# Stage ends of a one-core fp32 block: split weights a block ahead, last rows by halves of the tokens, 1/rms with priority, Sqrt's table loaded elsewhere

## The chip, the core and the metric

One NeuronCore of a Trainium2 chip runs the whole program. The time is device microseconds of one launch. The core's engines are PE (TensorE, matmuls; its weight loads are listed as PEld), DVE (VectorE), ACT (ScalarE), POOL (GpSimd) and SP (SyncE, which here issues DMAs). Each works through its own list of instructions in order, and waits where an operand of an instruction is not there yet.

## What is computed

Two layers on 256 latent tokens of width 2048. Layer 0 mixes tokens with a bidirectional RWKV-7 scan, which also reads 256 context tokens; layer 1 with a Hyena long convolution whose filters come from a small sine network. Behind each mixer and each MLP stands a root-mean-square norm, then the residual.

```python
def rms_norm(x, g):
    return x * lax.rsqrt(jnp.mean(x * x, axis=-1, keepdims=True) + NORM_EPS) * g

for i in range(2):
    h = modulate(rms_norm(x, norm_g[i, 0]), mod[:, 0], mod[:, 1])
    y = rwkv_mixer(h, hc, ...) if i == 0 else hyena_stream(h, ...)
    x = x + mod[:, 2] * rms_norm(y, norm_g[i, 1])
    h = modulate(rms_norm(x, norm_g[i, 2]), mod[:, 3], mod[:, 4])
    x = x + mod[:, 5] * rms_norm(squared_relu_mlp(h, mlp_up[i], mlp_down[i]), norm_g[i, 3])

# in hyena_filters, for L = 256 positions:
filt = (z @ f_w4).reshape(L, 2, HY_ORDER, D) * window
```

`rwkv_mixer` ends in a product with `w_o` (2048x2048), `hyena_stream` in one with `out_w`. `mod` is `silu(c) @ ada_w + ada_b`.

## The kernel before

All is fp32. Each operand of a product is split in two (ACT casts the high part, DVE subtracts for the low part; `split_into`), and each product is three matmuls (`mm3`: high·high, high·low, low·high). Names that end in h and l are these halves: `wh`, `wl` of a streamed weight, `w4h`, `w4l` of the filters' last weights, `hfh`, `hfl` of a filter block.

**Order of work.** The program is written as straight Python; every instruction is recorded (`call`, L53) and a scheduler then orders each engine's list from costs, dependencies and priorities. `tc.high_priority(n)` moves what stands in its block up by n. In the scan the order is pinned as written. Along time: projections (to about 600 us), the scan in eight groups (to 1421), `w_o` with its `resid` (to 1575), layer 0's MLP (to 2312) and `resid`, Hyena (to 2849) and `resid`, layer 1's MLP (to 3606) and `resid` to the output.

**Filters** (`filters`) fill PE's gaps in the scan's last group, 1290 to 1421. A unit is a column block dc (4 of 512) and an order o (2): eight units, 0 to 7. In a unit, for e = 0, 1 and token half tt = 0, 1: three matmuls of `zs`/`zd` with `w4` into an `sg` buffer; DVE multiplies by the window into `hf`; ACT casts `hfh`; DVE subtracts `hfl`; then `second` transforms them (matmuls with the DFT tables into `fl`), ACT copies `fl` to `ko`, SP stores `ko` to `spec`. The window of a column block (`win`, one buffer) is loaded for the next block when the last `hf` of a block is done. The weights of unit i are split when unit i begins.

**Streamed products.** `gemm_tok` computes 128 tokens by 512 columns per PSUM tile (column block n, token half tt), with K in blocks of four k; `w_o`, `mlp_down` and `out_w` use it. `evac` copies a tile to `o` (or adds to it; `y` in Hyena) on DVE, and `square_rows` sums its squares on ACT (`ysq`, into `ss`). `gemm_ws` has the weights' columns as output rows; in its lead mode four PSUM tiles share the K blocks, and `mlp_up` and Hyena's first product use it; there `evu` multiplies a tile by `rstd` into `nt`.

**resid** adds `ss` over n (DVE), takes Sqrt (ACT) and the reciprocal (DVE), and builds `dg`, a diagonal of 1/rms (DVE). PE multiplies `o` by `dg` (L450), which also transposes; `add` adds this to x and prepares the next stage's operands.

Beside all this `ada_run` computes `mod` from `ada_w` (`aw` tiles scaled on ACT, summed on POOL and DVE into `acc`), and `ada_scan` does some of it on PE in the scan, with the small tiles `wide` and `pick`.

Of the kernel before, what the change touches and what calls it, by code (L numbers as in the profile page):

```python
# [69 lines left out]
class Kern:  # L70
# [104 lines left out]
    def gemm_ws(self, W, K, ms, x, ntok, evac, lead=False):  # L175

        nk = K // P
        if lead:
            ps = [[self.mm.tile([P, 512], F32, name="mm") for _ in range(2)] for _ in range(2)]
            for k0 in range(0, nk, 4):  # L180
                w = [self.load_split(W[k0 * P : (k0 + 4) * P, m0 * P : (m0 + 2) * P].rearrange("(k p) n -> p k n", p=P), 4, 256)
                     for m0 in ms[:2]]
                for k in range(4):
                    for j in range(2):
                        for i in range(2):
                            self.mm3(ps[j][i][:, :ntok], self.cut(w[j][k], slice(i * P, (i + 1) * P)), x(k0 + k),
                                     k0 + k == 0, k0 + k == nk - 1)
                self.tick(self.rate)
            for j in range(2):
                for i in range(2):  # L190
                    evac(ms[j] + i, ps[j][i][:, :ntok])
            ms = ms[2:]
        for m0 in ms:
            ps = [self.mm.tile([P, 512], F32, name="mm") for _ in range(2)]
            for k0 in range(0, nk, 8):
                src = W[k0 * P : (k0 + 8) * P, m0 * P : (m0 + 2) * P].rearrange("(k p) n -> p k n", p=P)
                w = self.load_split(src, 8, 256)
                for k in range(8):
                    for i in range(2):
                        s = slice(i * P, (i + 1) * P)  # L200
                        self.mm3(ps[i][:, :ntok], self.cut(w[k], s), x(k0 + k),
                                 k0 + k == 0, k0 + k == nk - 1)
                self.tick(self.rate)
            for i in range(2):
                evac(m0 + i, ps[i][:, :ntok])

    def gemm_tok(self, W, x, evac, lead=False, stages=None):

        for ns in ((0, 1), (2,), (3,)) if lead else ((0,), (1,), (2,), (3,)):
            ps = {(n, tt): self.mm.tile([P, 512], F32, name="mm") for n in ns for tt in range(2)}  # L210
            for k0 in range(0, KT, 4):
                if stages and len(ns) > 1:
                    stages(k0)
                for n in ns:
                    w = self.load_split(W[k0 * P : (k0 + 4) * P, n * 512 : (n + 1) * 512].rearrange("(k p) n -> p k n", p=P), 4, 512)
                    for k in range(k0, k0 + 4):
                        for tt in range(2):
                            self.mm3(ps[n, tt], self.cut(x(k), slice(tt * P, (tt + 1) * P)), w[k - k0], k == 0, k == KT - 1)
                    self.tick(self.rate)
            for n in ns:  # L220
                for tt in range(2):
                    evac(n, tt, ps[n, tt])

    def square_rows(self, ss, y, n, tt, pool):

# [113 lines left out]
    def ada_scan(self, n, pool):  # L339


        nc = self.nc
        wide = pool.tile([P, KT, 32], F32, name="wide", bufs=1)
        nc.vector.memset(wide, 0.0)
        nc.vector.tensor_copy(wide[:, :, 0], self.sc2[:, 0, :])
        pick = pool.tile([P, 2], F32, name="pick", bufs=1)
        nc.vector.memset(pick, 0.0)
        for j in range(4):
            nc.vector.tensor_tensor(pick, pick, self.ident[:, 32 * j : 32 * j + 2], op=ALU.add)
        todo = [(layer, ch, i, half, k4) for layer, ch, i in itertools.islice(self.ada_todo, n) for half in range(2) for k4 in range(4)]  # L350

        def load(u):
            layer, ch, i, half, k4 = todo[u]
            w = pool.tile([P, 4, 256], F32, name="aw", bufs=2)
            c0 = ch * D + i * 512 + half * 256
            nc.sync.dma_start(w, self.I["ada_w"][layer, k4 * 512 : (k4 + 1) * 512, c0 : c0 + 256].rearrange("(a p) n -> p a n", p=P))
            return w

        def finish(layer, ch, i, half, ps):
            rows = pool.tile([P, 256], F32, name="rows", bufs=1)  # L360
            nc.scalar.copy(rows, ps)
            yield
            tp = self.sg.tile([P, 2, 2], F32, name="sg")
            for b in range(2):
                self.product(tp[:, b], rows[:, b * P : (b + 1) * P], pick, start=True, stop=True)
            c = 4 * i + 2 * half
            nc.vector.tensor_tensor(self.mod[:, layer, ch, c : c + 2], tp[:, :, 0], self.col("ada_b", layer * 96 + ch * 16 + c, 2), op=ALU.add)

        nxt = load(0)
        tail = iter(())  # L370
        for u, (layer, ch, i, half, k4) in enumerate(todo):
            w, nxt = nxt, load(u + 1) if u + 1 < len(todo) else None
            for _ in tail:
                pass
            if k4 == 0:
                ps = self.mm.tile([P, 256], F32, name="mm")
            for j in range(4):
                self.product(ps[32 * j : 32 * j + 32], wide[:, 4 * k4 + j, :], w[:, j], start=k4 == 0, stop=k4 == 3, tile_position=(0, 32 * j))
            if k4 == 3:
                tail = finish(layer, ch, i, half, ps)  # L380
                next(tail)
            yield
        for _ in tail:
            pass
# [40 lines left out]
    def resid(self, x, y, ss, layer, gi, ch, pool, nxt=None):  # L425
# [9 lines left out]
            for c in (L, L + 1):  # L435
                self.split_into(hi[:, :, c], self.mod[:, nxt[0], nxt[2], :], lo[:, :, c])

        for n in range(1, 4):
            nc.vector.tensor_tensor(ss[:, 0, :], ss[:, 0, :], ss[:, n, :], op=ALU.add)
        nc.scalar.activation(ss[:, 1, :], ss[:, 0, :], AF.Sqrt, bias=self.eps[:, 0:1], scale=1.0 / D)  # L440
        nc.vector.reciprocal(ss[:, 1, :], ss[:, 1, :])
        dg = pool.tile([P, 2, P], F32, name="dg", bufs=1)
        for tt in range(2):
            nc.vector.tensor_scalar(dg[:, tt], self.ident, ss[:, 1, tt : tt + 1], None, op0=ALU.mult)

        def add(k):
            pt = self.sg.tile([P, L], F32, name="sg")
# [30 lines left out]
    def filters(self, es):  # L478
# [46 lines left out]
        def load(i):  # L525
            dc, o = divmod(i, 2)
            if dc < 4:
                w4 = p2.tile([P, 512], F32, name="w4")
                for b in range(2):
                    c0 = (b * 2 + o) * D + dc * 512  # L530
                    nc.sync.dma_start(w4[64 * b : 64 * b + 64, :], I["f_w4"][0, :, c0 : c0 + 512])
                w4s.append(w4)
# [7 lines left out]
        def window(dc):  # L540
            if dc < 4:
                self.win = p2.tile([P, 2, 512], F32, name="win", bufs=1)
                nc.sync.dma_start(self.win, I["window"][:, dc * 512 : (dc + 1) * 512].rearrange("(a p) d -> p a d", p=P))

        window(0), load(0), skip(0)

        def first(dc, o, e, put):

            if not e:
                w4 = w4s.pop(0)  # L550
                self.w4 = split2(w4)
                load(2 * dc + o + 1)
            for tt in range(2):
                ps = self.sg.tile([P, 512], F32, name="sg")
                self.mm3(ps, self.cut(zz[e], slice(tt * P, (tt + 1) * P)), self.w4, True, True)
                hf = p2.tile([P, 512], F32, name="hf", bufs=3)
                nc.vector.tensor_tensor(hf, ps, self.win[:, tt, :], op=ALU.mult)
                if o and e and tt:
                    window(dc + 1)
                if e == 0 and tt == 0:  # L560
                    nc.vector.tensor_tensor(hf[0:1, :], hf[0:1, :], self.sk, op=ALU.add)
                    skip(2 * dc + o + 1)
                hh = p2.tile([P, 512], F32R, name="hfh", bufs=4)
                hfl = p2.tile([P, 512], F32R, name="hfl", bufs=4)
                put.append(self.split_into(hh[:], hf[:], hfl[:]))
                yield

        def split2(x):
            return self.split_into(p2.tile([P, 512], F32R, name="w4h")[:], x[:], p2.tile([P, 512], F32R, name="w4l")[:])

        def second(dc, o, e, hl):

# [851 lines left out]
    def rwkv_out(self, xp):  # L1424
        nc, tc = self.nc, self.tc
        with tc.tile_pool(reuse_waits="tile", name="oy", bufs=16) as oy, tc.tile_pool(reuse_waits="tile", name="op", bufs=1) as op:
# [7 lines left out]
            o = {(n, tt): op.tile([P, 512], F32, name=f"o{n}{tt}") for n in range(4) for tt in range(2)}  # L1434
            ss = op.tile([P, 4, 2], F32, name="ss")

            def ev(n, tt, ps):
                nc.vector.tensor_copy(o[n, tt], ps)
                self.square_rows(ss, o, n, tt, op)
# [43 lines left out]
            self.resid(x, o, ss, layer, 3, 5, mp, None if layer else (1, 0, 0))  # L1483

    AW = 6
    PRT = 1
    PRA, PRH = 100, 200
    MIXV = 3
    XB = 3
# [7 lines left out]
    PRI, PRJ = 200, 100  # L1497
    NEGV = 0
    SLACK = 0
    PRB = 200  # L1500
    LPOOL = 2
    FX = 3
# [332 lines left out]
```

## Time and profile before

| | |
|---|---|
| median of 3 runs | 3630.55 us (3610.51 to 3632.46) |
| profiled execution, its own time | 3626.62 us |
| its span, first to last instruction | 3623.9 us |
| mean granted TensorE clock | 0.965 |
| PE busy | 3349.5 us, 92% of the span |
| DVE, ACT, POOL busy | 2474.2 (68%), 1740.7 (48%), 551.9 us (15%) |
| DMA | 836.78 MB, mean 231 GB/s |

Shares are of the span. A time such as 1428.56 is counted from the span's start. A wait names the instruction that stood still and what released it; the engine behind a `<-` is that releaser.

### The profile page before, as it was taken

How to read it: one execution, taken by the hardware profiler on the slowest of the kernel's cores; microseconds unless marked ns; L12 is line 12 of the kernel's file. 1: busy time of each engine (PE TensorE's matmuls, PEld its weight loads, DVE VectorE, ACT ScalarE, POOL GpSimd, SP SyncE). 2: the span in 40 equal slices, each digit the busy share in tenths (PEclk: the TensorE clock that was granted, in tenths of full speed). 3: DMA queues.
4: the chain of work that ended last, by engine and by line, in shares of the span. 5: the costliest groups of instructions: out<-in, count | busy, mean ns of one | idle time of the engine just before them, and what ended most of it. 6: DMA issues, size and time to landing. Idle time of an engine off the chain costs nothing. (4 is left out here: it accounts for less than half of the span.)

```text
span 3623.9 us, 74582 instructions
## 1 busy us (share of the span) xinstructions
PE 3349.5 (92%) x30598; PEld 2912.4 (80%) x30598; DVE 2474.2 (68%) x3787; ACT 1740.7 (48%) x3069; POOL 551.9 (15%) x576
## 2 busy tenths in 40 slices
PE   7798877989999878999999999999999899999999
PEld 3376666878888756798988889899997798989897
DVE  5888675777777755587777776587787685555554
ACT  4444344444554544444434335576564664435343
POOL 2632221111111000000000002044441540000000
PEclk9989988999999989999999999999999999999999
DMA  9668798888899735688888887476665776555553
GB/s 328 203 211 268 238 293 253 272 267 272 272 281 276 224 126 168 202 257 288 255 271 277 283 264 240 158 238 214 213 211 176 241 251 197 178 189 182 192 181 126
DMA packets 587806, 836.78 MB, mean 231 GB/s; under 512 B 39551, under 2 KB 373280, under 8 KB 587464
## 3 DMA queue, kind: packets, MB, share of 16 engines
q1 hardware_dynamic: 556360, 718.76, 62.0%
q0 software_dynamic: 31104, 113.26, 9.9%
q8 instruction: 239, 3.92, 0.4%
q14 instruction: 103, 0.84, 0.1%
HBM read 777.31 MB, written 54.59 MB: 230 GB/s over the span
## 5 line engine op out<-in xcount | busy, mean ns | idle before, releaser
L53 DVE TENSOR_TENSOR wl<-w,wh 128x1024 fp32r<-128x1024 f32 (+1 forms) x716 | 919.6, 1290 | 541.1 <-ACT wh L53 537.8
L53 ACT CAST wh<-w 128x1024 fp32r<-128x1024 f32 (+1 forms) x716 | 737.7, 1043 | 728.8 <-PE mm L111 416.4
L111 PE MATMUL mm<-hxh,wh 128*128 128x258 f32 x2816 | 805.3, 287 | 13.2 <-DVE nt L53 11.4
L111 PE MATMUL mm<-hxh,wl 128*128 128x258 f32 x2816 | 803.9, 286 | 5.5 <-DVE wl L53 5.5
L111 PE MATMUL mm<-hxl,wh 128*128 128x258 f32 x2816 | 801.1, 285 | 0.0
L111 PEld LDWEIGHTS mm<-hxh,wh 128*128 128x128 f32 x2816 | 536.3, 191 | 17.4 <-DVE nt L53 13.5
L111 PEld LDWEIGHTS mm<-hxh,wl 128*128 128x128 f32 x2816 | 536.0, 190 | 8.5 <-DVE wl L53 7.2
L111 PEld LDWEIGHTS mm<-hxl,wh 128*128 128x128 f32 x2816 | 538.6, 191 | 1.8
L322 POOL TENSOR_TENSOR acc<-acc,aw 128x512 f32<-128x512 f32 x180 | 274.2, 1523 | 1360.7 <-ACT aw L53 1259.3
L111 PE MATMUL mm<-wh,uh 128*128 128x512 f32 x1024 | 405.8, 396 | 1.2 <-DVE nt L53 1.2
L111 PE MATMUL mm<-wl,uh 128*128 128x512 f32 x1024 | 400.2, 391 | 4.0 <-DVE wl L53 4.0
L111 PE MATMUL mm<-wh,ul 128*128 128x512 f32 x1024 | 402.6, 393 | 0.0
L53 DVE SCALAR_TENSOR_TENSOR acc<-aw,sc,acc 128x512 f32<-128x512 f32 x300 | 233.4, 778 | 101.0 <-DMA aw<-in_ada_w 98.5
L111 PEld LDWEIGHTS mm<-wl,uh 128*128 128x128 f32 x1024 | 192.6, 188 | 49.0 <-DVE wl L53 6.2
L111 PEld LDWEIGHTS mm<-wh,ul 128*128 128x128 f32 x1024 | 192.2, 188 | 45.6
L111 PEld LDWEIGHTS mm<-wh,uh 128*128 128x128 f32 x1024 | 192.6, 188 | 42.3 <-DVE nt L53 1.8
L111 PE MATMUL fl<-fh,fx 128*128 128x256 f32 x1024 | 213.1, 297 | 10.1 <-DMA fx<-xv 8.6
L111 PEld LDWEIGHTS fl<-fh,fx 128*128 128x128 f32 x1024 | 168.6, 194 | 28.1 <-issue 14.1
L53 ACT ACTIVATE aw<-aw,sc 128x512 f32<-128x512 f32 x180 | 125.7, 719 | 130.7 <-DMA aw<-in_ada_w 129.6
L111 PE MATMUL fl<-flo,fx 128*128 128x256 f32 x512 | 146.4, 286 | 0.0
L111 PE MATMUL mm<-xh,wh 128*128 128x512 f32 (+1 forms) x320 | 126.8, 416 | 17.5 <-ACT xh L53 14.1
L111 PE MATMUL sg<-ard,KB 64*64 64x64 f32 (+1 forms) x3584 | 130.4, 247 | 11.2 <-DVE NT L53 3.7
(352 smaller groups left out, 6016.3 us busy)
## 6 DMA issues: line engine op xcount, KB each, us to landing
aw<-in_ada_w SPq DMA_DIRECT2D x288, 512.0 KB, 5.7
w<-in_mlp_down SPq DMA_DIRECT2D x128, 1024.0 KB, 5.2
w<-in_mlp_up SPq DMA_DIRECT2D x120, 1024.0 KB, 6.1
fx<-xv POOLq DMA_DIRECT2D x128, 512.0 KB, 6.2
aw<-in_ada_w SPq DMA_DIRECT2D x192, 256.0 KB, 3.1
w<-in_hy_in_w SPq DMA_DIRECT2D x44, 1024.0 KB, 5.9
fx<-xr POOLq DMA_DIRECT2D x64, 512.0 KB, 5.8
w<-in_w_k SPq DMA_DIRECT2D x16, 1024.0 KB, 5.7
```

What stands on the lines that cost most here:

```text
L53: return self.kern.pin(self.key, f(*a, **kw))
L111: return self.pin("pe", self.nc.tensor.matmul(out, lhsT=lhsT, rhs=rhs, **kw))
L322: nc.gpsimd.tensor_tensor(acc, acc, w[:, a], op=ALU.add)
```

## The change

1. `gemm_ws`, lead mode: the last K block goes through the column pairs one after the other instead of k by k.
2. `gemm_tok`: the last K block does all of token half 0, then all of half 1; where the tile is the last column block (n = 3), `evac` is under priority `PRT`.
3. `resid`: `ss` sums, Sqrt, reciprocal and `dg` are under priority `PRT`, which goes from 1 (used nowhere) to 400.
4. `ada_scan`: the set-up of `wide` and `pick` is under priority `PRS` = 1000.
5. `filters`: the weights of the next unit are split behind the last `hf` of the unit before, and their load is issued a unit further ahead.
6. `rwkv_out`: one activation Sqrt on a small constant (`st`) stands ahead of the `w_o` product.

```diff
@@ gemm_ws
-                for k in range(4):
-                    for j in range(2):
-                        for i in range(2):
-                            self.mm3(ps[j][i][:, :ntok], self.cut(w[j][k], slice(i * P, (i + 1) * P)), x(k0 + k),
-                                     k0 + k == 0, k0 + k == nk - 1)
+                order = [(j, k) for k in range(4) for j in range(2)]
+                for j, k in sorted(order) if k0 == nk - 4 else order:
+                    for i in range(2):
+                        self.mm3(ps[j][i][:, :ntok], self.cut(w[j][k], slice(i * P, (i + 1) * P)), x(k0 + k),
+                                 k0 + k == 0, k0 + k == nk - 1)
@@ gemm_tok
-                    for k in range(k0, k0 + 4):
-                        for tt in range(2):
-                            self.mm3(ps[n, tt], self.cut(x(k), slice(tt * P, (tt + 1) * P)), w[k - k0], k == 0, k == KT - 1)
+                    pairs = [(k, tt) for k in range(k0, k0 + 4) for tt in range(2)]
+                    for k, tt in sorted(pairs, key=lambda p: p[1]) if k0 == KT - 4 else pairs:
+                        self.mm3(ps[n, tt], self.cut(x(k), slice(tt * P, (tt + 1) * P)), w[k - k0], k == 0, k == KT - 1)
                     self.tick(self.rate)
-            for n in ns:
-                for tt in range(2):
-                    evac(n, tt, ps[n, tt])
+            with self.tc.high_priority(self.PRT if 3 in ns else 0):
+                for n in ns:
+                    for tt in range(2):
+                        evac(n, tt, ps[n, tt])
@@ ada_scan
+        with self.tc.high_priority(self.PRS):
+            nc.vector.memset(wide, 0.0)
+            nc.vector.tensor_copy(wide[:, :, 0], self.sc2[:, 0, :])
+            nc.vector.memset(pick, 0.0)
...
@@ resid
         dg = pool.tile([P, 2, P], F32, name="dg", bufs=1)
+        with self.tc.high_priority(self.PRT):
+            for n in range(1, 4):
+                nc.vector.tensor_tensor(ss[:, 0, :], ss[:, 0, :], ss[:, n, :], op=ALU.add)
+            nc.scalar.activation(ss[:, 1, :], ss[:, 0, :], AF.Sqrt, bias=self.eps[:, 0:1], scale=1.0 / D)
+            nc.vector.reciprocal(ss[:, 1, :], ss[:, 1, :])
+            for tt in range(2):
+                nc.vector.tensor_scalar(dg[:, tt], self.ident, ss[:, 1, tt : tt + 1], None, op0=ALU.mult)
@@ filters
-        window(0), load(0), skip(0)
+        def weights(i):
+            halves.append(split2(w4s.pop(0)))
+            load(i)
...
+        window(0), load(0), load(1), skip(0)
+        halves = []
+        weights(2)
 
         def first(dc, o, e, put):
 
             if not e:
-                w4 = w4s.pop(0)
-                self.w4 = split2(w4)
-                load(2 * dc + o + 1)
+                self.w4 = halves.pop(0)
...
                 if o and e and tt:
                     window(dc + 1)
+                if e and tt and w4s:
+                    weights(2 * dc + o + 3)
@@ rwkv_out
+            nc.scalar.activation(op.tile([P, 2], F32, name="st"), self.eps, AF.Sqrt)
+
@@ constants
-    PRT = 1
+    PRT = 400
+    PRS = 1000
```

How the lists of instructions move is seen at three places. First ACT in the filters, from unit 0's last `hfh` to unit 1's first; `rhs`, `KR` and `sqo` belong to the scan beside it. Before:

```order
L53 COPY ko<-fl 128x512
L53 CAST hfh<-hf 128x512
L53 COPY rhs<-sc 128x256
L53 COPY KR<-sg 128x4x64 x2
L53 ACTIVATE sqo<-dv 128x256
L53 COPY ko<-fl 128x512
L53 CAST w4h<-w_17082 128x512
L53 CAST hfh<-hf 128x512
```

and changed:

```order
L53 COPY ko<-fl 128x512
L53 CAST w4h<-w_17076 128x512
L53 CAST hfh<-hf 128x512
L53 COPY rhs<-sc 128x256
L53 COPY KR<-sg 128x4x64 x2
L53 ACTIVATE sqo<-dv 128x256
L53 COPY ko<-fl 128x512
L53 CAST hfh<-hf 128x512
```

The cast of the next unit's weights went up past that unit boundary's copies and one `hfh`; on DVE `w4l` went up in the same way, between the last `hf` and its `hfl`. It is so in units 1 to 7; unit 0's split stands where it stood.

Second, ACT around `w_o`, from the filters' last copies to the start of `resid` (`yh` are the halves of w_o's tokens); one piece of the difference at each end:

```order
 L53 COPY ko<-fl 128x512 x3
+L53 ACT_TABLE_LOAD
+L53 ACTIVATE st<-eps 128x2
 L53 CAST yh<-yt 128x256 x8
 L53 CAST wh<-w 128x1024
...
 L53 ACTIVATE ysq,ss<-o_18599 128x512
 L53 ACTIVATE ysq,ss<-o_18600 128x512
-L53 ACT_TABLE_LOAD
 L53 ACTIVATE ss<-ss,eps 128x2
 L53 ACTIVATE hxh<-x,gs 128x256
```

The table load went from ahead of `resid`'s Sqrt to ahead of `w_o`; the order between is that of before.

Third, ACT at the end of Hyena, up to `resid`'s Sqrt; the `wh` are weights of layer 1's first `mlp_up` product, the `aw` those of `mod`. Before:

```order
L53 CAST wh<-w 128x1024
L53 ACTIVATE acc<-aw,sc_92 128x512
L53 ACTIVATE aw<-aw,sc_92 128x512
L53 CAST wh<-w 128x1024
L53 ACTIVATE aw<-aw,sc_92 128x512 x2
L53 ACTIVATE ysq,ss<-y 128x512
L53 CAST wh<-w 128x1024
L53 ACTIVATE ysq,ss<-y 128x512
L53 ACTIVATE aw<-aw,sc_92 128x512 x2
L53 ACTIVATE ss<-ss,eps 128x2
```

and changed:

```order
L53 CAST wh<-w 128x1024 x2
L53 ACTIVATE acc<-aw,sc_92 128x512
L53 ACTIVATE aw<-aw,sc_92 128x512 x3
L53 CAST wh<-w 128x1024
L53 ACTIVATE ysq,ss<-y 128x512
L53 CAST wh<-w 128x1024
L53 ACTIVATE ysq,ss<-y 128x512
L53 ACTIVATE aw<-aw,sc_92 128x512 x2
L53 ACTIVATE ss<-ss,eps 128x2
```

One `wh` stands behind the three `aw` instead of between them; on SP the second of the `aw` loads there now stands ahead of a `mlp_up` load instead of behind it.

## Rows read from the trace of the kernel before

**Rows 1.** The page's first part: busy us (share of the span) and instructions of each engine.

```profile
PE 3349.5 (92%) x30598; PEld 2912.4 (80%) x30598; DVE 2474.2 (68%) x3787; ACT 1740.7 (48%) x3069; POOL 551.9 (15%) x576
```

**Rows 2.** PE's waits from 1425 to the end, by what released them: engine, its operation and line, what it waited for, us in total, times, longest us.

```profile
PE sg L450 <- DVE dg L53: 21.4, 4, 10.0
...
PE mm L111 <- DVE nt L53: 12.5, 10, 2.9
PE mm L111 <- ACT yh L53: 7.4, 1, 7.4
```

**Rows 3.** Busy us of each engine in five stretches (the stretch, its length, busy us of PE, PEld, DVE, ACT and POOL with instructions, granted clock, DMA share, GB/s): the filters beside the scan's last group, two parts of that stretch, the handover to w_o, the rest of layer 1's MLP.

```profile
1290.00:1421.00 131.00, 113.71 (x1220) 85.32 (x1221) 70.36 (x127) 61.98 (x133) 0.00 (x0) 0.92 0.35 115
1330.00:1350.00 20.00, 17.39 (x198) 13.69 (x200) 9.43 (x18) 8.49 (x18) 0.00 (x0) 0.83 0.34 115
1350.00:1390.00 40.00, 35.43 (x454) 26.59 (x446) 20.92 (x37) 19.08 (x42) 0.00 (x0) 1.00 0.45 142
1421.00:1429.00 8.00, 0.63 (x6) 0.50 (x4) 1.52 (x7) 1.02 (x3) 0.00 (x0) 0.83 0.74 232
2910.00:3600.00 690.00, 689.84 (x4353) 625.33 (x4352) 395.72 (x461) 321.87 (x462) 35.75 (x23) 1.00 0.59 190
```

**Rows 4.** PE's waits from 1290 to 1429, same columns as Rows 2.

```profile
PE sg L111 <- ACT w4h L53: 14.8, 7, 6.0
PE sg L111 <- DVE w4l L53: 1.4, 6, 0.2
```

**Rows 5.** PE in order of time at the first matmul of units 2, 3, 4 and 6 (start, us, engine, line, operation, tile written and read, shape, count, and in brackets the idle time before it and what ended it).

```profile
1324.02 0.49 PE L111 MATMUL sg<-w4h,zsh 128*128 128x512 f32 x1 [1.15 <-DVE KR L53]
...
1337.89 0.80 PE L111 MATMUL sg<-w4h,zsh 128*128 128x512 f32 x1 [2.61 <-ACT w4h L53]
...
1358.10 0.49 PE L111 MATMUL sg<-w4h,zsh 128*128 128x512 f32 x1 [1.19 <-ACT w4h L53]
...
1390.26 0.49 PE L111 MATMUL sg<-w4h,zsh 128*128 128x512 f32 x1 [1.24 <-ACT w4h L53]
```

**Rows 6.** ACT, then DVE, in order of time between units 2 and 3; the columns are those of Rows 5.

```profile
1334.67 0.62 ACT L53 CAST hfh<-hf 128x512 fp32r<-128x512 f32 x1 [1.24 <-DVE hf L53]
1336.73 0.58 ACT L53 COPY ko<-fl 128x512 f32<-128x512 f32 x1 [1.44 <-DMA spec<-ko]
1337.21 0.62 ACT L53 CAST w4h<-w 128x512 fp32r<-128x512 f32 x1
...
1335.32 0.69 DVE L53 TENSOR_TENSOR hfl<-hf,hfh 128x512 fp32r<-128x512 f32 x1 [0.69 <-ACT hfh L53]
```

**Rows 7.** DVE's first `hf` of units 4 and 6, and SP's issue of the window load for unit 4, in order of time on each engine.

```profile
1360.27 0.69 DVE L53 TENSOR_TENSOR hf<-sg,win 128x512 f32<-128x512 f32 x1 [1.50 <-DMA win<-in_window]
...
1394.34 0.69 DVE L53 TENSOR_TENSOR hf<-sg,win 128x512 f32<-128x512 f32 x1 [3.40 <-DMA win<-in_window]
...
1354.56 0.38 SPq L53 DMA_DIRECT2D win<-in_window  x1
```

**Rows 8.** ACT at the handover from the filters to w_o.

```profile
1428.56 1.02 ACT L53 CAST yh<-yt 128x256 fp32r<-128x256 f32 x3 [6.17 <-DMA yt<-y]
```

**Rows 9.** PE early in w_o.

```profile
1452.62 0.73 PE L111 MATMUL mm<-wh,yh 128*128 128x512 f32 x2 [3.05 <-ACT wh L53]
```

**Rows 10.** ACT at the end of w_o.

```profile
1526.54 1.04 ACT L53 CAST wh<-w 128x1024 fp32r<-128x1024 f32 x1 [1.51 <-DMA w<-in_mlp_up]
...
1528.98 1.28 ACT L53 ACT_TABLE_LOAD   x1
1530.27 0.30 ACT L53 ACTIVATE ss<-ss,eps 128x2 f32<-128x2 f32 x1
```

**Rows 11.** DVE, then ACT, at the end of layer 0's MLP.

```profile
2313.20 1.23 DVE L53 TENSOR_TENSOR wl<-w,wh 128x1024 fp32r<-128x1024 f32 x1 [0.30 <-ACT wh L53]
2314.57 0.16 DVE L53 TENSOR_TENSOR ss<-ss 128x2 f32<-128x2 f32 x1 [0.15 <-ACT ysq L53]
...
2314.77 0.29 ACT L53 ACTIVATE ss<-ss,eps 128x2 f32<-128x2 f32 x1 [0.23 <-DVE ss L53]
```

**Rows 12.** PE's first matmul of `resid` at the four ends: w_o, layer 0's MLP, Hyena, layer 1's MLP.

```profile
1531.15 1.65 PE L450 MATMUL sg<-dg,o 128*128 128x128 f32 x6 [5.21 <-DVE dg L53]
...
2315.64 0.60 PE L450 MATMUL sg<-dg,o 128*128 128x128 f32 x3 [3.56 <-DVE dg L53]
...
2858.57 1.65 PE L450 MATMUL sg<-dg,y 128*128 128x128 f32 x6 [9.96 <-DVE dg L53]
...
3608.88 1.16 PE L450 MATMUL sg<-dg,o 128*128 128x128 f32 x8 [2.70 <-DVE dg L53]
```

**Rows 13.** ACT, then SP's DMA issues, at the end of Hyena.

```profile
2847.60 1.05 ACT L53 CAST wh<-w 128x1024 fp32r<-128x1024 f32 x1 [1.35 <-DMA w<-in_mlp_up]
2851.43 0.72 ACT L53 ACTIVATE aw<-aw,sc 128x512 f32<-128x512 f32 x1 [2.78 <-DMA aw<-in_ada_w]
...
2846.91 0.37 SPq L53 DMA_DIRECT2D aw<-in_ada_w  x1
2847.38 0.41 SPq L53 DMA_DIRECT2D w<-in_mlp_up  x1
```

**Rows 14.** DVE at the start of layer 0's MLP.

```profile
1572.37 1.75 DVE L53 RECIPROCAL rstd<-rstd 128x256 f32<-128x256 f32 x1
...
1574.61 0.42 DVE L53 TENSOR_TENSOR nt<-mm,rstd 128x256 f32<-128x256 f32 x1
```

More of the change, by code (lines that the diff above doesn't have):

```diff
@@ L343, in ada_scan @@
         wide = pool.tile([P, KT, 32], F32, name="wide", bufs=1)
-        nc.vector.memset(wide, 0.0)
-        nc.vector.tensor_copy(wide[:, :, 0], self.sc2[:, 0, :])
         pick = pool.tile([P, 2], F32, name="pick", bufs=1)
-        nc.vector.memset(pick, 0.0)
-        for j in range(4):
-            nc.vector.tensor_tensor(pick, pick, self.ident[:, 32 * j : 32 * j + 2], op=ALU.add)
+        with self.tc.high_priority(self.PRS):
+            nc.vector.memset(wide, 0.0)
+            nc.vector.tensor_copy(wide[:, :, 0], self.sc2[:, 0, :])
+            nc.vector.memset(pick, 0.0)
+            for j in range(4):
+                nc.vector.tensor_tensor(pick, pick, self.ident[:, 32 * j : 32 * j + 2], op=ALU.add)
         todo = [(layer, ch, i, half, k4) for layer, ch, i in itertools.islice(self.ada_todo, n) for half in range(2) for k4 in range(4)]
@@ L436, in resid @@
                 self.split_into(hi[:, :, c], self.mod[:, nxt[0], nxt[2], :], lo[:, :, c])
[L438 to L441, printed above, removed]
         dg = pool.tile([P, 2, P], F32, name="dg", bufs=1)
-        for tt in range(2):
-            nc.vector.tensor_scalar(dg[:, tt], self.ident, ss[:, 1, tt : tt + 1], None, op0=ALU.mult)
+        with self.tc.high_priority(self.PRT):
[5 more added lines that the diff above has]
+                nc.vector.tensor_scalar(dg[:, tt], self.ident, ss[:, 1, tt : tt + 1], None, op0=ALU.mult)
         def add(k):
@@ L543, in window, with split2 @@
                 nc.sync.dma_start(self.win, I["window"][:, dc * 512 : (dc + 1) * 512].rearrange("(a p) d -> p a d", p=P))
-        window(0), load(0), skip(0)
+        def weights(i):
+            halves.append(split2(w4s.pop(0)))
+            load(i)
+        def split2(x):
+            return self.split_into(p2.tile([P, 512], F32R, name="w4h")[:], x[:], p2.tile([P, 512], F32R, name="w4l")[:])
+        window(0), load(0), load(1), skip(0)
+        halves = []
+        weights(2)
         def first(dc, o, e, put):
             if not e:
-                w4 = w4s.pop(0)
-                self.w4 = split2(w4)
-                load(2 * dc + o + 1)
+                self.w4 = halves.pop(0)
             for tt in range(2):
@@ L566, in first @@
                 yield
-        def split2(x):
-            return self.split_into(p2.tile([P, 512], F32R, name="w4h")[:], x[:], p2.tile([P, 512], F32R, name="w4l")[:])
         def second(dc, o, e, hl):
```

## The prediction

> **What bounds the kernel now.** I read the page's busy shares first: PE works 92% of the span, so time can only be won where PE stands idle or runs at a lower granted clock [rows 1]. From late in layer 1's MLP nothing is to be had: in 690.00 us PE is busy 689.84 [rows 3]. Then I read PE's waits by what released them, over the stretches that the change touches. After the scan the longest group is the four waits for `dg`, the diagonal of 1/rms on which `resid` begins, 21.4 us together with 10.0 the longest; ten for `nt` make 12.5, one for `yh` 7.4 [rows 2]. In the last group of the scan, where the filters run, seven waits for `w4h` make 14.8 us, the longest 6.0, and six for `w4l` 1.4 [rows 4]. Over 1290 to 1421 PE is busy 113.71 of 131.00 us and DVE and ACT only 70.36 and 61.98 [rows 3], so PE's order is the limit there and a wait that goes is mostly time won, if nothing else is late at the same spot. These are the places where the change can act; the question is at each what comes late next.
>
> **Filters' weights a unit ahead.** A unit is one pair (dc, o): eight in all. The first unit's 6.0 us wait is the start of the filters' matmuls and stays: the order of ACT and DVE is the same there. Seven units are left. In each, `w4h` now stands ahead of the previous unit's last `hfh` on ACT, `w4l` ahead of its `hfl` on DVE. What they cost there: before such an `hfh` ACT sat idle 1.24 us for `hf`, and the `w4h` cast takes 0.62, so it fits; DVE sat idle 0.69 before `hfl`, and `w4l` takes 0.69 [rows 6]. So I book nothing for the new place. If that cover were gone, as when `w4h` is not yet ready at that point, it would be 0.62 to 0.69 us for each of seven units, 4.8 at most. No instruction is added, and SP issues the same loads, each one spec store earlier, behind the window load where there is one.
>
> What is won, unit by unit: the seven waits without the first are 14.8 − 6.0 = 8.8 us, and the ones for `w4l` 1.4, together 10.2 [rows 4]. Three units have something else that is late. Unit 2 waited 1.15 us for `KR`, DVE's copy that frees its PSUM buffer, and keeps that [rows 5]. Units 4 and 6 are the first of a new column block, and there DVE's first `hf` waits for the window's load, by 1.50 and 3.40 us after all else was ready; the load has one buffer and is issued only behind the previous block's last `hf`, at 1354.56 for an `hf` at 1360.27 [rows 7]. Earlier weights leave that load where it is. So 1.19 + 1.24 us [rows 5] and two `w4l` waits (two of six, about 0.5) move from the weights to the window: 2.9. That leaves 10.2 − 2.9 = 7.3 us. Unit 3 is the largest single piece, 2.61 us [rows 5]: ACT stood 1.44 us in `ko`, which waited for a spec store, ahead of `w4h` [rows 6]; the cast now stands before that `ko`. Behind this stall the granted clock was 0.83 over 1330 to 1350, against 1.00 in the 40 us after [rows 3]. If the fall came from the stall, up to 0.17 × 20 = 3.4 us more come back; if it came from the thin stretch of the scan's matmuls, none. I take 0.7, a fifth, since no row here tells the two apart. Forecast for the filters: −8.0, between −3 (PE's other waits there, for `hf` and `hfh`, take the place of more than half) and −10.7 (7.3 + 3.4).
>
> **Between filters and w_o.** PE stands 7.4 us for `yh` [rows 2], busy 0.63 us in the 8.00 from 1421 [rows 3], and ACT 6.17 us for the load `yt` that feeds it [rows 8]. This chain starts with the last spec stores and moves with the filters' end, neither longer nor shorter. The dummy Sqrt and its table load go onto ACT right here, ahead of the `yh` casts: 1.28 us of load and one tiny activation (0.30, as the Sqrt at w_o's end) [rows 10] inside 6.17 of waiting. Nothing is booked; without that cover it would be 1.6.
>
> **End of w_o.** Here ACT did: `wh` at 1526.54 after 1.51 us for its weights' load, two `ysq`, the table load from 1528.98 for 1.28, Sqrt from 1530.27 [rows 10]. With the load gone from this place the Sqrt waits for the last `ss` add on DVE; two or three tenths of a us stay of the 1.28, as layer 0's MLP end shows: `ss` from 2314.57, Sqrt 0.20 later, ACT idle 0.23 for it [rows 11]. I take −0.9, between −0.8 and −1.28. The Trainium skill, "ScalarE: Activation LUTs", section "What ACT_TABLE_LOAD costs", puts a switch at about 1.28 us of load and 1.38 of drain, 2.66 in all; by that this edit would be worth up to 1.4 us more. The trace shows the load and no drain: `ysq` ends at its start and Sqrt starts at its end, so the row decides. The order of the halves does nothing for w_o: both `ysq` still stand behind the `wh` that waits for its load.
>
> At w_o's start PE waits 3.05 us for a `wh` whose load had come late [rows 9]; SP now issues one `w_o` load ahead of a `mlp_up` load. Nothing shows which of the queue's loads was late by how much, so 0 to −1.5 (half of that wait); I take −0.5.
>
> **Ends of the two MLPs and of Hyena.** With halves, the first tokens' rows are done 12 matmuls before the last, and `ysq` for them runs under the rest. But the last half's chain is then what counts: `o`, `ysq`, `ss`, Sqrt, reciprocal, `dg`, one behind the other. At the end of layer 1's MLP nothing stands between the links already, and PE waits 2.70 us [rows 12]; only the first `ysq`'s overlap is won there: −0.1. At layer 0's MLP DVE did a `wl` at 2313.20 for 1.23 us and only then `ss` at 2314.57 [rows 11]; that `wl` still stands ahead of `ss`, so −0.2, between −0.9 (as if it were gone: 3.56 against 2.70 us [rows 12]) and 0. At Hyena's end the priority does least: ACT waited 2.78 us for an `aw` load at 2851.43 ahead of the first `ysq` [rows 13]. That `aw` still stands there, and the `wh` that ran at 2847.60 now stands behind it, 1.05 us more ahead of `ysq`. Loads are permuted too: an `aw` load that SP could issue only at 2846.91, when its buffer came free, now has the next `mlp_up` load behind it rather than ahead. I take +1.0; a gain of up to 5 (half of the 9.96 [rows 12]) would need `aw` to land before ACT reaches it, a loss of 4 that a `wh` waits for the displaced load.
>
> **Start of layer 0's MLP.** The lead's last block by pairs of column tiles lets the first pair's rows be read earlier. But `nt` needs `rstd`, whose reciprocal ran on DVE from 1572.37 for 1.75 us, and `nt` came at 1574.61 [rows 14]. PE's 2.9 us wait for it [rows 2] is set by `rstd`, not by the matmuls. In the new order one `wl` (1.23 [rows 11]) stands between `rstd` and the first `nt`: between +1.2 and 0, I take +0.8. The set-up of `wide` and `pick` under priority changes no engine's order: 0.
>
> **Sum.** −8.0 − 0.9 − 0.5 − 0.1 − 0.2 + 1.0 + 0.8 = −7.9 us. The profiled execution took 3626.6, so 3618.7; the median of the three runs lies 3.9 above that execution, so 3618.7 to 3622.6 for a median: I give **3620**.
>
> **Rivals.** (a) *The filters give little.* The stall goes, but PE then waits for `hfh` and `hfl` of the units that it reached sooner. For it speaks that DVE was waiting for ACT's `hfh` each time and that a late window eats two units already; against it that DVE and ACT have half their time free. Filters −3, the rest as above: 3626.6 − 2.9 = 3623.7, 3624 to 3628 for a median. (b) *More comes back.* The clock keeps its higher level (−2.7 more), the `aw` at Hyena's end lands in time (−5 instead of +1.0), the MLP's end gains 0.7 more: −7.9 − 2.7 − 6.0 − 0.7 = −17.3, so 3609 to 3613. Against it stands that the order still has the waiting `aw` ahead. (c) *Slower, by loads in the way of 1/rms.* At Hyena's end two `wh` now stand around the first `ysq`, behind the `aw`, and their `mlp_up` loads are issued behind it on SP. If each lands 4 us later than its turn on ACT, the end is 8 us later rather than 1.0. The rest of the change gives −8.9, so this alone decides from 8.9; together with filters at their low end (−3) it decides from 3.9, and at 8 the total is +4.1: 3631 to 3635. For it speaks that ACT and DVE run in order; against it that the load at 2847.38 would have some 5 us to land. (d) *The change does not do what it says.* For the priority on `ss` and the set-up this is so by the order; it is in the sum as nearly nothing.
>
> **How the numbers follow.** Forecast (−4 to −12): 0.56; (a): 0.18; (b): 0.14; (c): 0.12. The range from 3601 to 3633 leaves out the far half of (b) and of (c); it allows for the 22 us between the three runs before only in part. One per cent, 36 us, is about what a measurement of this kernel can tell from no change; no case comes near it, and only misread stretches would: faster 0.03, within 0.95, slower 0.02.
>
> **What would show it.** In the changed trace: no wait for `w4h` over 0.3 us except the first, `hf` in units 4 and 6 still waiting for the window, unit 3's clock; no table load at w_o's end and `dg` there 4.3 us late instead of 5.2; waits for `dg` of about 3.4, 11 and 2.6 at the other ends; PE's wait for the first `nt` near 3.7. I am wrong if the filters' stretch is not 6 us shorter, or if Hyena's end moves by more than 3 us either way.

## The result and the profile after

The changed kernel took 3603.55 us (median of 10 runs, 3587.07 to 3614.70), the kernel before 3617.15 over its ten runs (3604.60 to 3632.46). The medians differ by 13.6 us; the ratio taken over the runs is 0.9948, 95% interval 0.9927 to 0.9970, which is 18.8 us less, between 10.9 and 26.4. The forecast was 7.9 us less for an execution and 3620 as the time. The direction was right and the range holds the time, but the size was less than half of the 18.8 and lies below the interval, and the time stands on a base (3620 + 7.9 = 3627.9) that is 10.7 us above the median of ten.

The page's first line of the changed kernel answers to [rows 1]:

```profile
PE 3338.0 (93%) x30598; PEld 2904.4 (81%) x30598; DVE 2472.1 (69%) x3787; ACT 1739.2 (48%) x3070; POOL 549.9 (15%) x576
```

PE's waits around the filters, changed kernel, answer to [rows 4] (its columns); this kernel comes to unit 0 at 1285.69 us:

```profile
PE mm L111 <- ACT yh L53: 7.6, 1, 7.6
PE sg L111 <- ACT w4h L53: 6.0, 1, 6.0
...
PE sg L111 <- DVE hf L53: 0.9, 1, 0.9
...
PE sg L111 <- DVE w4l L53: 0.2, 1, 0.2
```

Of the seven waits for `w4h` only the first is left, and of six for `w4l` one; `yh` is as before. The two profiled executions, cut at PE's first matmul of unit 0, of `w_o`, of `resid` at the four ends, and at the end of the span (us each; the time from unit 0 to `w_o` is called the filters' stretch below):

| | to unit 0 | filters, to w_o | w_o, to dg | to dg, MLP 0 | to dg, Hyena | to dg, MLP 1 | to the end |
|---|---|---|---|---|---|---|---|
| before | 1294.58 | 134.44 | 102.13 | 784.49 | 542.93 | 750.31 | 15.02 |
| changed | 1285.69 | 120.29 | 97.78 | 788.70 | 543.42 | 750.54 | 15.38 |

The 8.9 us ahead of unit 0 can't be put down to the change: up to there PE has the same matmuls in both, DVE, ACT and POOL the same instructions in the same order, and on SP only `sk` moved, behind two loads of filter weights, among the last five. In the profiled executions below unit 0 came at 1288.31 to 1300.78 in the six with the old loads there (1294.2 in the mean) and at 1282.15 to 1293.31 in the eight with edit 5's (1287.8), four of these with the window's load in two. The two ranges overlap; whether edit 5 has a part in the difference stays open. So a single pair of executions tells a total only within some 10 us, and what follows is read stage by stage. Of what is left, −13.2 us, the filters have −14.15; w_o's −4.35 and the MLP's +4.21 cancel, and neither is clear of the spread: over all the executions below these two stages took 97.8 to 102.1 and 780.9 to 788.7 us.

The filters' stretch, without its last 8 us of handover (columns: stretch, its length, PE busy us with matmuls, granted clock with 1.00 for 2.4 GHz, DMA share, GB/s). Before:

```profile
1294.58:1421.02 126.44, 113.73 (x1220) 0.94 0.36 118
```

and changed:

```profile
1285.69:1397.98 112.29, 107.34 (x1222) 0.98 0.41 133
```

PE's idle time went from 12.71 to 4.95 us, 7.8 less; its busy time for the same matmuls went from 113.73 to 107.34, 6.4 less. The forecast had 7.3 for the first and 0.7 for the second.

The ends, changed kernel, PE's rows that answer to [rows 12], with the first wait for `nt` between the first two:

```profile
1503.76 1.65 PE L453 MATMUL sg<-dg,o 128*128 128x128 f32 x6 [4.28 <-DVE dg L53]
...
1552.87 0.55 PE L111 MATMUL mm<-hxh,wh 128*128 128x258 f32 x1 [4.61 <-DVE nt L53]
...
2292.46 1.16 PE L453 MATMUL sg<-dg,o 128*128 128x128 f32 x8 [3.36 <-DVE dg L53]
...
2835.88 1.44 PE L453 MATMUL sg<-dg,y 128*128 128x128 f32 x5 [7.38 <-DVE dg L53]
...
3586.42 1.16 PE L453 MATMUL sg<-dg,o 128*128 128x128 f32 x8 [2.64 <-DVE dg L53]
```

5.21, 3.56, 9.96 and 2.70 us became 4.28, 3.36, 7.38 and 2.64; the wait for `nt` went from 2.9 [rows 2] to 4.61. ACT at the handover and at w_o's end, which answers to [rows 8] and [rows 10]:

```profile
1398.95 1.28 ACT L53 ACT_TABLE_LOAD   x1
...
1405.52 1.32 ACT L53 CAST yh<-yt 128x256 fp32r<-128x256 f32 x4 [5.08 <-DMA yt<-y]
...
1497.28 1.05 ACT L53 CAST wh<-w 128x1024 fp32r<-128x1024 f32 x1 [2.15 <-DMA w<-in_mlp_up]
...
1501.94 0.63 ACT L53 ACTIVATE ysq<-o 128x512 f32<-128x512 f32 x1
...
1502.89 0.29 ACT L53 ACTIVATE ss<-ss,eps 128x2 f32<-128x2 f32 x1 [0.23 <-DVE ss L53]
```

The table load lies ahead of a 5.08 us wait for `yt`, and Sqrt follows the second `ysq` with 0.23 us of idle time for `ss`.

### The profile page after: what moved, and what is told of

Same layout as the page of the kernel before. It is cut to its first block, busy times and chain, and to the rows that moved or that the text cites. A ratio compares the mean times of both kernels' runs of the same rounds, so it can differ in the third digit from the quotient of the medians.

```text
span 3601.8 us, 74591 instructions
## 1 busy us (share of the span) xinstructions
PE 3338.0 (93%) x30598; PEld 2904.4 (81%) x30598; DVE 2472.1 (69%) x3787; ACT 1739.2 (48%) x3070; POOL 549.9 (15%) x576
## 3 DMA queue, kind: packets, MB, share of 16 engines
q8 instruction: 239, 3.92, 0.5%
## 4 chain that ended last, share of the span: by engine, by line
PE 48%; DMA 21%; DVE 14%; issue 7%; ACT 6%; POOL 3%; SPq 0%; ACTq 0%; POOLq 0%; DVEq 0%
PE mm L111 34%; DMA aw<-in_ada_w 9%; PE fl L111 5%; PE sg L111 5%; PE sc L111 3%; DVE wl L53 3%; DMA w<-in_mlp_up 2%; POOL acc L323 2%; DMA w<-in_mlp_down 2%; DVE acc L53 2%; ACT wh L53 2%; DVE xt L53 1%; DVE tmp L53 1%; ACT aw L53 1%; DVE d L53 1%
## 5 line engine op out<-in xcount | busy, mean ns | idle before, releaser
L53 DVE SCALAR_TENSOR_TENSOR acc<-aw,sc,acc 128x512 f32<-128x512 f32 x300 | 231.9, 773 | 104.4 <-DMA aw<-in_ada_w 102.1
```

Of the source, the lines that this page charges most:

```text
L53: return self.kern.pin(self.key, f(*a, **kw))
```

## Experiments

Theory A: the gain sits in the filters, and its size is more than the idle time because a long wait of PE is followed by a lower clock. Rival B: the clock is a matter of the execution, and the other edits carry part of the gain.

**Edit 5 alone, and all but it.** `f_only` is the kernel before with the diff's part in `filters`; `no_filters` is the changed kernel without it.

> Edit 5 alone (filters' weights split a unit ahead), all else as before. Theory A: the whole gain sits in the filters; from unit 0's first matmul to w_o's first the stretch goes from 134.4 us to about 120.3 as in the changed kernel, half of it as PE's idle time (20.1 to 12.5) and half as a granted clock of 1.00 instead of 0.83 behind unit 3's stall; the total falls by 12 to 15 us. Rival B: the clock is a matter of the execution and the other edits carry part of the gain; then the stretch shortens by 7 to 8 us and the total by no more than 9.

> All edits but 5 (lead order, halves, priorities, Sqrt's table ahead of w_o), filters as before. Theory A: the filters' stretch stays at 134 us; the 0.9 us of the table load is won at w_o's end, and lost again at the start of layer 0's MLP, where a low half now stands ahead of the first nt; total within 3 us of before. Rival B: these edits are worth 4 to 6 us, since in the changed kernel w_o was 4.4 us shorter.

Edit 5 alone: 3602.27 against 3614.61 us, ratio 0.9968 (0.9951 to 0.9985), 11.6 us less, 5.4 to 17.7; stretch 120.13 us. All but it: 3614.91, ratio 0.9996 (0.9980 to 1.0012), 1.4 us less, from 7.2 less to 4.3 more; stretch 129.64. The total's 11.6 is just under the 12 to 15 of theory A, which lie within its interval. The gain sits in the filters, and what the other five edits do is not told from nothing by the time. The stretch of 129.64, with the filters as before, was not expected, and its row shows why:

```profile
1288.31:1409.95 121.64, 109.41 (x1220) 0.98 0.38 122
```

Idle time is 12.23 us, as before; but the clock did not fall, and PE was busy 109.41 us instead of 113.73. For `f_only`:

```profile
1284.78:1396.91 112.13, 106.73 (x1219) 0.97 0.41 132
```

5.40 us idle, 106.73 busy. So 2.7 us of busy time go even where the clock was the same. They show in the rows at a unit's start. Before, unit 1 (last matmul of the unit ahead, then `w4h`, `w4l`, `w4h`):

```profile
1307.20 0.40 PE L111 MATMUL fl<-hfh,dftcl 128*128 128x512 f32 x1
1308.79 0.49 PE L111 MATMUL sg<-w4h,zsh 128*128 128x512 f32 x1 [1.19 <-ACT w4h L53]
1309.51 0.50 PE L111 MATMUL sg<-w4l,zsh 128*128 128x512 f32 x1 [0.23 <-DVE w4l L53]
1309.85 0.39 PE L111 MATMUL sg<-w4h,zsl 128*128 128x512 f32 x1
```

and changed:

```profile
1298.31 0.39 PE L111 MATMUL fl<-hfh,dftcl 128*128 128x512 f32 x1
1298.54 0.40 PE L111 MATMUL sg<-w4h,zsh 128*128 128x512 f32 x1
1298.77 0.39 PE L111 MATMUL sg<-w4l,zsh 128*128 128x512 f32 x1
1299.00 0.40 PE L111 MATMUL sg<-w4h,zsl 128*128 128x512 f32 x1
```

From the first to the fourth of these matmuls it was 2.65 us before and 0.69 after, 1.96 less, where the waits in brackets sum to 1.42. The two matmuls behind the waits last 0.49 and 0.50 us; in the stream they last 0.40 and 0.39, and each starts 0.23 behind the last. So this pair of waits costs about 0.5 us beyond its brackets, and the trace books it as busy time.

**Unit 3 alone, and all units but 3.** The split is made ahead only for the units named, and the loads stay where they were:

```diff
             if not e:
-                w4 = w4s.pop(0)
-                self.w4 = split2(w4)
-                load(2 * dc + o + 1)
+                u = 2 * dc + o
+                self.w4 = halves.pop(u) if u in halves else split2(w4s.pop(0))
+                load(u + 1)
...
+                if e and tt and 2 * dc + o + 1 in (3,):
+                    halves[2 * dc + o + 1] = split2(w4s.pop(0))
```

with `(3,)` in one and `(1, 2, 4, 5, 6, 7)` in the other.

> Only unit 3's weights are split ahead, the other six units as before, loads as before. Theory A: the 2.6 us stall and the low clock behind it go together, so the filters' stretch is 5 to 7 us shorter, with a clock of 0.95 or more in the 20 us behind unit 3's first matmul. Rival B: the clock falls there anyway; 2 to 3 us shorter, clock about 0.83 there.

> Units 1, 2 and 4 to 7 ahead, unit 3 as before. Theory A: unit 3's stall and the 0.83 behind it stay; the stretch is 7 to 9 us shorter than before. Rival B: 5 us shorter, and whether the clock falls behind unit 3 is chance.

Unit 3 alone: stretch 127.83 us, 6.6 less than in the execution of before, but only 1.8 less than `no_filters`, whose clock had not fallen; clock 1.00 behind unit 3. All but 3: 124.77, 9.7 less, with a wait and a clock at unit 3 as in these rows; PE's first matmul of unit 3:

```profile
1342.53 0.57 PE L111 MATMUL sg<-w4h,zsh 128*128 128x512 f32 x1 [3.23 <-ACT w4h L53]
```

and the 20 us from there:

```profile
1342.53:1362.53 20.00, 19.84 (x237) 0.91 0.44 142
```

Unit 3 alone came within theory A's 5 to 7 us, though the 6.6 holds only against an execution in which the clock fell. All but 3 came above its 7 to 9 and far above rival B's 5. That the fall at unit 3 is chance, which rival B had too, these two executions alone do not exclude.

**The clock behind a wait.** `late_unit5` is `f_only`, except that unit 5's weights are split at unit 5's start behind four more casts of the same tile, which makes PE wait at a place where no execution so far had a lower clock. `before_again` is another execution of the kernel before.

```diff
             if not e:
+                if 2 * dc + o == 5:
+                    w4 = w4s.pop(0)
+                    hi = p2.tile([P, 512], F32R, name="w4h")
+                    for _ in range(4):
+                        nc.scalar.copy(hi, w4)
+                    halves.append(self.split_into(hi[:], w4[:], p2.tile([P, 512], F32R, name="w4l")[:]))
+                    load(7)
                 self.w4 = halves.pop(0)
...
-                if e and tt and w4s:
+                if e and tt and w4s and 2 * dc + o != 4:
```

> As f_only, but unit 5's weights are split at its own start as before, behind four repeats of the same cast on ACT (0.62 us each), so PE waits about 3.5 us there, at a place where no other run had a low clock. Theory A (the clock falls behind a wait of 2.6 us or more): a granted clock of 0.80 to 0.93 in the 20 us behind unit 5's first matmul, and the filters' stretch 120.1 + 3.5 + 2 to 4 = 126 to 128 us. Rival B (the fall belongs to unit 3's place or to the execution): clock 1.00 there, stretch 123 to 124.

> The kernel before, looked at once more. Theory A: the clock behind unit 3's first matmul goes with that unit's wait for w4h: under 2 us of wait 1.00 and a stretch of about 129.5, over 2.5 us 0.8 to 0.9 and about 134. Rival B: no such pairing. The time up to unit 0 will again differ by several us from the 1294.6 of the first look, with the same instructions.

`late_unit5`, ACT's five casts ahead of unit 5:

```profile
1352.78 3.24 ACT L53 CAST w4h<-w 128x512 fp32r<-128x512 f32 x5
```

PE then:

```profile
1356.07 0.79 PE L111 MATMUL sg<-w4h,zsh 128*128 128x512 f32 x1 [3.92 <-ACT w4h L53]
```

and the 20 us from there:

```profile
1356.07:1376.07 20.00, 20.00 (x225) 0.86 0.38 124
```

The stretch was 126.46 us, as theory A had it. The matmul behind the 3.92 us wait lasts 0.79, twice the 0.39 of the stream: the lower of the two levels, 1.2 GHz, and the mean over the next 20 us is 0.86. Now `before_again`, PE at unit 3:

```profile
1338.80 0.79 PE L111 MATMUL sg<-w4h,zsh 128*128 128x512 f32 x1 [2.10 <-ACT w4h L53]
```

and the 20 us from there:

```profile
1338.80:1358.80 20.00, 18.57 (x223) 0.91 0.44 144
```

the same of `no_filters`, which has the same filters:

```profile
1330.77 0.51 PE L111 MATMUL sg<-w4h,zsh 128*128 128x512 f32 x1 [1.75 <-ACT w4h L53]
```

and the 20 us from there:

```profile
1330.77:1350.77 20.00, 18.35 (x228) 1.00 0.48 155
```

the 20 us in the execution of before, behind the 2.61 us wait of [rows 5]:

```profile
1337.89:1357.89 20.00, 19.02 (x220) 0.84 0.38 121
```

and the changed kernel's, where no wait is left there:

```profile
1323.43:1343.43 20.00, 19.51 (x270) 1.00 0.61 198
```

and `table_only`'s, an execution of the next experiment with the same filters as before, PE at unit 3 and the 20 us from there:

```profile
1338.27 0.80 PE L111 MATMUL sg<-w4h,zsh 128*128 128x512 f32 x1 [3.70 <-ACT w4h L53]
...
1338.27:1358.27 20.00, 18.58 (x223) 0.92 0.43 144
```

Waits of 2.10, 2.61, 3.23, 3.70 and 3.92 us were each followed by a lower clock, at unit 3 or, where the wait was made there, at unit 5; with 1.75, and without a wait, it stayed at 1.00. (2.10 lies between the two cases that were expected of `before_again`.) But the length of a wait does not decide it. In the three executions with the old filters in which the clock fell at unit 3 it fell a second time: in the execution of before behind the 1.24 us wait at unit 6 ([rows 5]; the two parts of the stretch in [rows 3] end ahead of it, at 1390), and in `before_again` and `table_only` behind a wait of 1.32 us at unit 5. The 20 us from those units' first matmuls, in this order, and last the same wait of 1.32 us in `no_filters`, where nothing fell:

```profile
1390.26:1410.26 20.00, 18.31 (x174) 0.91 0.29 105
...
1374.40:1394.40 20.00, 18.30 (x219) 0.91 0.47 158
...
1373.87:1393.87 20.00, 18.31 (x219) 0.91 0.49 161
...
1365.19:1385.19 20.00, 18.22 (x224) 1.00 0.48 161
```

And early in `w_o` a wait of 2.23 us in the changed kernel was followed by no fall:

```profile
1427.66 0.73 PE L111 MATMUL mm<-wh,yh 128*128 128x512 f32 x2 [2.23 <-ACT wh L53]
...
1427.66:1447.66 20.00, 19.48 (x85) 1.00 0.68 233
```

That the waits bring the falls is shown all the same: `late_unit5` has a fall where a wait was put in, `f_but_3` has one at unit 3 and, with the waits at units 5 and 6 gone, no other, and in the seven executions with every unit split ahead, those of the later experiments among them, the clock was 1.00 from unit 1 to 8 us ahead of `w_o`. Which wait is followed by a fall does not come out of these rows.

Unit 3's wait depends on when a spec store lands: `ko` waits for it ahead of `w4h`, 1.44 us in the execution of before [rows 6], 0.94 in `before_again`, 0.58 in `no_filters`, 2.13 in `table_only`, and PE then waited 2.61, 2.10, 1.75 and 3.70. So the kernel before paid for a lower clock in some executions and not in others. The stretch before was 134.44, 132.57, 129.64 and, in the next experiment, 134.45 us: 132.8 in the mean; changed it was 120.29, 120.13 and, below, 120.65. That is 12.4 us. The rows of the three that are not shown above, `before_again`, `table_only` and `after_again`, without the last 8 us:

```profile
1296.02:1420.59 124.57, 112.42 (x1224) 0.95 0.37 120
...
1293.84:1420.29 126.45, 111.91 (x1220) 0.96 0.37 118
...
1289.00:1401.65 112.65, 106.78 (x1219) 0.98 0.41 132
```

PE's idle time is 12.9 us before and 5.4 changed, in the mean: 7.5 of the 12.4. The other 4.9 are busy time, 111.9 against 107.0. With `no_filters`, where the clock did not fall, as the level between them (109.41), half of that, 2.5 us, is what the waits cost beyond their brackets, and 2.5 is clock in the mean of four executions (0 to 4.3).

**The table load alone, and the changed kernel once more.** `table_only` has the one line with `st`.

> Edit 6 alone (Sqrt's table loaded ahead of w_o). PE's wait for dg at w_o's end 4.2 to 4.3 us instead of 5.2, the waits at the other three ends as before (3.6, about 10, 2.7), w_o's begin not later. If the table switch had a drain that the trace hides, the wait would be 3 us or less.

> The changed kernel, looked at once more. The filters' stretch 120 to 121 us with a clock of 1.00 behind unit 3's first matmul; dg at Hyena's end about 7.5 us, if what was won there comes from the order of loads (aw issued before two mlp_up loads), or anywhere from 7 to 10 if it was chance; the first nt's wait 4.0 to 4.8.

`table_only`, PE at w_o's end:

```profile
1530.01 1.22 PE L450 MATMUL sg<-dg,o 128*128 128x128 f32 x4 [4.22 <-DVE dg L53]
```

4.22 us, so one switch is worth 1.0 us, and no drain shows. The other three waits were as before (3.56, 10.28, 2.70). `after_again`: stretch 120.65, `nt` 4.8 us, and at Hyena's end:

```profile
2833.56 1.86 PE L453 MATMUL sg<-dg,y 128*128 128x128 f32 x7 [9.63 <-DVE dg L53]
```

9.63 us with the instructions that gave 7.38 in the other execution, where about 7.5 was expected if the order decides alone. In the other execution, with 7.38, ACT's rows and SP's issue of the second `aw` load were:

```profile
2828.68 1.34 ACT L53 ACTIVATE aw<-aw,sc 128x512 f32<-128x512 f32 x2 [2.99 <-DMA aw<-in_ada_w]
2830.50 1.05 ACT L53 CAST wh<-w 128x1024 fp32r<-128x1024 f32 x1 [0.49 <-DMA w<-in_mlp_up]
...
2824.79 0.37 SPq L53 DMA_DIRECT2D aw<-in_ada_w  x1
```

PE's last matmul had ended at 2828.50 (2835.88 − 7.38). So `aw` was there 0.18 us behind it and its load had been issued 3.7 us ahead, where before it was 2.82 behind and 1.7 ahead ([rows 13], with 2848.61 from [rows 12]). In `after_again`, with the same order, the load was issued only 2.7 us ahead (2821.19 against 2823.93), and its `aw` came 1.35 behind (2825.28). The wait at Hyena's end was 7.38, 7.92, 7.43 and 9.63 us with the changed order there, and 9.34 to 10.44 with the old one (the order of `no_filters` and `no_lead_win` is the old one at this place). So the order won some 2 us in three of four executions, and in one nothing; it goes with how early the load was issued, and what delayed it in that one was not tried.

**The window by token halves.** Since unit 2, 4 and 6 still wait for the window, it is made of two tiles, each loaded behind its own last use; nothing else is changed.

```diff
-        def window(dc):
-            if dc < 4:
-                self.win = p2.tile([P, 2, 512], F32, name="win", bufs=1)
-                nc.sync.dma_start(self.win, I["window"][:, dc * 512 : (dc + 1) * 512].rearrange("(a p) d -> p a d", p=P))
+        win = [None, None]
+
+        def window(dc, tt):
+            if dc < 4:
+                win[tt] = p2.tile([P, 512], F32, name=f"win{tt}", bufs=1)
+                nc.sync.dma_start(win[tt], I["window"][tt * P : (tt + 1) * P, dc * 512 : (dc + 1) * 512])
...
-                if o and e and tt:
-                    window(dc + 1)
+                if o and e:
+                    window(dc + 1, tt)
```

> Edit 5 alone, and the window of a column block in two tiles by token half, each loaded as soon as its own half is free, so the first half's load is issued one hf earlier and is half as long. In f_only DVE waits for the window at units 2, 4 and 6, some 9 us together. If PE is held by that: the stretch from unit 0 to w_o 3 to 6 us shorter than 120.1. If PE has other work beside it: within 1.5 us of 120.1, and the time that of f_only.

> All edits, and the window by halves. If the window holds PE, 3 to 6 us less than the changed kernel (ratio to before about 0.9935); otherwise that of the changed kernel, 0.995 to 0.997.

> All edits but 1 (the lead's order as before), and the window by halves. The first nt now stands ahead of a wl again: its wait 2.8 to 4.0 us instead of 4.0 to 4.8. In this order one wh stands ahead of the waiting aw at Hyena's end, as before: dg there 9.5 to 10.4 if the order decides, 7.4 to 7.9 if it does not. The time within 3 us of the kernel with all edits and the window by halves.

> All edits and the window by halves, once more on this chip beside the run without edit 1: ratio to before 0.993 to 0.996, the stretch from unit 0 to w_o 115 to 117 us.

With edit 5 the stretch is 116.15 us, 4.0 less:

```profile
1293.09:1401.24 108.15, 106.04 (x1221) 0.98 0.42 138
```

2.11 us idle instead of 5.40: the window held PE for 3.3 us. With all edits it is 115.69 and 115.98. Ratios to before: 0.9963 (0.9950 to 0.9976) with edit 5; 0.9949 (0.9929 to 0.9969) and, in the second run, 0.9944 (0.9927 to 0.9961) with all; 0.9951 (0.9932 to 0.9970) without edit 1. The last two, on one chip, are 3596.88 and 3597.39 us against 3618.64. All with the window in halves is the best version here by its stretch, 4.5 us; the times of the versions do not tell it from the changed kernel's 0.9948, where about 0.9935 was expected.

Without edit 1, PE at the start of layer 0's MLP:

```profile
1555.56 0.58 PE L111 MATMUL mm<-hxh,wh 128*128 128x258 f32 x1 [1.58 <-DVE nt L53]
```

1.58 us of wait for `nt`, less than the 2.8 to 4.0 expected, where the order with edit 1 had 4.6, 4.0, 4.8, 4.8 and, in the last run, 3.2. Yet the time from `dg` at w_o's end to `rstd`'s reciprocal was 44.74 us there, as in the executions with edit 1 (42.97 to 45.71); in the eight without edits 1 to 4 it was 41.22 to 44.54, 42.9 in the mean. The ranges overlap. The 1.8 us between the means, ahead of `rstd`, are not edit 1's by this execution; which of the others moves a load there was not tried.

## Why the prediction was right and where not

**The filters' idle time** was right: 7.3 us forecast, 7.5 in the mean. So was the step on its own cover, `w4h` and `w4l` at their new places cost nothing, and the one on units 4 and 6: DVE still waits for the window (9.1 us in three waits instead of 4.9 in two), and taking that wait away gave 3.3 us of idle time, about the 2.9 that the working had left out.

**The filters' total** was wrong, 8.0 against 12.4 in the mean and 14.15 between the two profiled executions. Two terms of the step "unit by unit" were too small. A wait was priced at its bracket, and what it costs beyond, 2.5 us in all, was left out, though [rows 5] show 0.49 for the first matmul behind it and the stream's pace of 0.23 could be read beside it. And the clock's return, for which 0.7 of 3.4 was taken "since no row here tells the two apart", was 2.5 in the mean and up to 4.3 in an execution. The value taken lay nearer to no effect with nothing to speak for that end, and the second fall, behind unit 6, was not looked at. Rival (b), which had the clock's return in it, was nearer to the result in its sum (−17.3), but by luck: its largest item, −5 at Hyena's end, came at half of that in one execution and at nearly nothing in another, and the −0.7 at the MLP's end did not come.

The filters' 12.4 us leave some 6 of the 18.8 without a stage. `f_only`, with the filters' edit alone, took 11.6 less, and the interval of the 18.8 reaches down to 10.9, so the runs show no other stage that the sum missed; the time ahead of unit 0 stays open.

**The place of the sum.** 3620 was made from the profiled execution, 3626.6, and a median of three runs, 3630.55; its base is 3627.9, and ten runs gave 3617.15. That is 10.7 of the 16.5 us by which the forecast lies above the measured median; the 13.6 us between the medians, against 7.9, make the rest. No reading of the profile could mend the base; the forecast had to allow for it in its range, and the lower end did.

**The ends.** w_o's end: −0.9 forecast, −0.9 between the profiled executions and −1.0 in `table_only`; the row decided rightly. The Trainium skill, "ScalarE: Activation LUTs", section "What ACT_TABLE_LOAD costs", gives 2.66 us for a switch, which these rows do not bear out. w_o's start: −0.5 forecast; PE's wait for the first late `wh` was 3.05 us before and 2.23 in the changed kernel, but 1.52 to 3.14 over the executions with edits and without, so nothing is shown there. MLP 0: −0.2, measured −0.2. MLP 1: −0.1, measured −0.06. Hyena: +1.0 forecast, −2.6 in one execution and −0.3 in another: the sign was wrong. The step that failed took the issue of the `aw` load as fixed, at 2846.91 when its buffer came free, 1.7 us ahead of PE's last matmul; in the new order the load was issued 3.7 us ahead where the 2.6 were won, which outweighs the `wh` that now stands behind it. `nt`: +0.8 forecast; 2.6 to 4.0 us with the old order, 3.2 to 4.8 with edit 1, 1.2 more in the mean, the length of the one `wl`. `no_lead_win`, with a `wl` no longer ahead of `nt`, had 1.58: the direction is the step's, but the drop is more than a `wl`, and the rest of it is not explained.

**Rival (c)** did not come: the `wh` at Hyena's end waited 0.49 us for its load, not 4. **Rival (a)** neither: behind the waits that went, PE waited for `hf` 0.9 us once.

## What to carry to other kernels

Price a wait on PE at more than its bracket: read the start-to-start time from the last matmul ahead of it to the first that runs at the stream's pace again, and look at the clock behind it: in some executions waits of 1.2 to 3.9 us were followed by a lower clock, in others waits of 1.3 to 2.3 us were not, so read several executions. Splitting an operand one block ahead, into the idle time that another engine's cast leaves, removed such waits here, with ACT and DVE busy for half of the time, and no wait of PE for the moved work came of it beyond 0.2 us. Where executions differ by more than the change, compare stage by stage between fixed instructions, and take the baseline from more than three runs.

## What was not expected of the hardware

A wait of 2.10 us was followed by a matmul of 0.79 us instead of 0.39, and one of 1.75 was not; but waits of 1.24 and 1.32 us were followed by a lower clock in three executions, and one of 2.23 was not. At the higher clock the first matmul behind a wait of 1.2 to 1.75 us lasted 0.49 to 0.51 us, not 0.39. And the time to unit 0 differed by 18.6 us between executions whose instructions there are the same but for the order of SP's last few loads.
